# Gated outputs of two head groups parked in DRAM, and a key pair projected ahead of a gate, in a four-group decoder trunk

## The chip, the cores and the metric

One core of one Trainium2 chip runs the whole kernel. The time is in device microseconds of one launch. Each version was run three times; the median counts. The engines are called as in the profile: PE (TensorE), DVE (VectorE), ACT (ScalarE), POOL (GpSimd) and SP (SyncE, which issues all of this kernel's DMAs).

## The reference

Two layers, batch 1, 1024 tokens, 1024 channels. Each layer projects its input once, runs four groups of heads on slices of that projection, normalises each group's output, multiplies it by a gate and projects back:

```python
def hybrid_layer(x, pos, g_pre, w_in, sinks, conv_w, conv_b, g_cq, w_uq, g_ckv, w_ukv, g_grp, w_out, g_post):
    b, s, _ = x.shape
    h = rmsnorm(x, g_pre) @ w_in
    (a_q, a_k, a_v, b_b, b_c, b_x, c_q, c_kv, c_kr, d_q, d_k, d_v, gate) = jnp.split(h, SPLIT_IDX, axis=-1)
    ya = swa_sink_attention(...)          # A: sliding window, 4 heads of 64, 2 key heads
    yb = short_gated_conv(b_b, b_c, b_x, conv_w, conv_b)   # B: width 3, 256 channels
    yc = mla(c_q, c_kv, c_kr, pos, g_cq, w_uq, g_ckv, w_ukv)   # C: causal softmax, 4 heads
    yd = stick_breaking_attention(...)    # D: 4 heads of 64
    y = jnp.stack([ya, yb, yc, yd], axis=2)
    y = rmsnorm(y, g_grp.reshape(N_GROUPS, GROUP_WIDTH)).reshape(b, s, D_MIX)
    y = y * jax.nn.silu(gate)
    return x + rmsnorm(y @ w_out, g_post)

# D, for a block of 128 queries
z = einsum(q, k) * scale
log_keep = where(mask, log_sigmoid(-z), 0.0)
after = cumsum(log_keep, reverse=True) - log_keep
a = where(mask, exp(log_sigmoid(z) + after), 0.0)
out = einsum(a, v)
```

All of it is float32. Group D's cumulative sum along the keys is what makes its weights costly outside the matmuls.

## The kernel before, in words

A product in float32 is made of three passes: each operand is split into a rounded part (an ACT copy) and the rest (a subtraction on DVE or POOL), and PE multiplies high by high, high by low and low by high. A projection chunk, such as the 128 columns DK1 (the keys of D's second head pair), has 48 matmuls of 512 columns: two halves Q of 512 tokens, 8 slices of 128 input channels, three passes. The keys to what stands in such names: AQ, AK and AV are queries, keys and values of A, and likewise for D; G10 and G11 are the two 128-column chunks of group B's gate (groups are numbered A 0, B 1, C 2, D 3).

D's work comes in tasks, one for a head and 256 queries: scores into a bank `sc` (with a mask product), ACT's exponentials, on DVE a scan along the keys and a product with the break weights, for two query blocks each. Then PE transposes the weights into a bank `tr`, ACT copies their high and DVE subtracts their low part into a PT tile, and PE multiplies the values with it into the one bank `pv`.

The program is emitted by a planner (class `Weaver`). Each stage is a Python generator, here called a stream: `gemm()` (L1626) emits the projections, `scores()` the scores, `pvs()` the transposes and the products with values, `norms()` the group norms, `z_parts()` and `z_split` (L1487) the split of the gated outputs for the last projection, `w_out_rows()` the load of that projection's weights, and `outs()` the projection. A stream yields a condition: `need(...)` waits for a mark of another stream, `room(n)` for n free tiles, `W.when(...)` for the planned time at which data is there. `run()` goes on with the first stream in its list that could start by the planned present, else with the earliest. PE runs in the order of emission. On ACT, DVE, POOL and for SP's issues the planner keeps a list of planned slots, puts each instruction into the first hole that fits, and ties neighbours together, so that every engine has one fixed order.

SBUF tiles come from pools with fixed numbers: 34 `g` tiles of 4 KB per partition (activations, keys, outputs, split weights), 6 `P`, 3 `PT`, 3 weight tiles `W`, 2 `raw` buffers for weights that arrive, 3 `t`, 4 `f`. PSUM has 3 banks `sc`, 2 `tr`, 1 `pv` and 2 `w`.

In a layer the stream of projections goes: C's columns, B (all of it), DV, DQ0, DK0, C's gate (two chunks), DQ1, B's first gate chunk G10, DK1, G11, then A's AV, AQ0, AK0, AQ1, D's gate, A's gate. The order in which the weights arrive is a list of its own (L714 to L717), and has to be the same. `gate` (L1180) multiplies a group's normed output `L["y"][grp][Q]` by its gate in place on POOL. B's convolution output goes through DRAM (`yBd`) until its norm and again until its gate; C's, D's and A's outputs stay in SBUF. Each output tile holds one half Q of the tokens and takes one `g` tile; C's and B's four gated tiles are held until `z_split` rounds and splits them for the last projection.

Names in the profile: a tile or bank has its tag behind an x (`xg`, `xP`, `xPT`, `xsc`); `xw` is both the bank `w` and a weight tile `W`. All of ACT's, DVE's and POOL's instructions pass through one helper line, L85; matmuls are L479, transposes (as a product with `ident`) L483, DMA issues L396.

## Time and profile before

| | before |
|---|---|
| median of 3 runs | 1173.47 us (1171.46 to 1174.13) |
| the profiled execution's own time | 1172.81 us |
| its span, first to last instruction | 1171.0 us |
| mean granted clock of TensorE | 0.995 |
| instructions | 17883 |
| D's second pair, layer 0 | 321.2 to 408.5 us |
| D's second pair, layer 1 | 897.9 to 985.1 us |

The span lies within the time; 1.8 us are ahead of the first and behind the last instruction. "Busy" of PE counts each matmul from its start to its modelled end; neighbours overlap. The granted clock is a share of TensorE's full speed; it has two levels, 2.4 GHz (1.00) and 1.2 GHz (0.50), and a mean over a stretch lies between them.

### The profile page before, as it was taken

How to read it: one execution, taken by the hardware profiler on the slowest of the kernel's cores; microseconds unless marked ns; L12 is line 12 of the kernel's file. 1: busy time of each engine (PE TensorE's matmuls, PEld its weight loads, DVE VectorE, ACT ScalarE, POOL GpSimd, SP SyncE). 2: the span in 40 equal slices, each digit the busy share in tenths (PEclk: the TensorE clock that was granted, in tenths of full speed). 3: DMA queues.
4: the chain of work that ended last, by engine and by line, in shares of the span. 5: the costliest groups of instructions: out<-in, count | busy, mean ns of one | idle time of the engine just before them, and what ended most of it. 6: DMA issues, size and time to landing. Idle time of an engine off the chain costs nothing.

```text
span 1171.0 us, 17883 instructions
## 1 busy us (share of the span) xinstructions
PE 1142.7 (98%) x6302; PEld 978.2 (84%) x6302; DVE 822.9 (70%) x1685; ACT 640.1 (55%) x1443; POOL 347.9 (30%) x477
## 2 busy tenths in 40 slices
PE   8999999999999999999999999999999999999997
PEld 6988888987787788878889888899878877888886
DVE  6868687549969878852764777873688788888323
ACT  7665566246556667631454655651655565675211
POOL 4225143116224235310221332420353332451000
PEclk9999999999999999999999999999999999999999
DMA  6121202121111011321451122021201111124123
GB/s 227 36 64 33 68 19 60 50 81 27 27 37 37 18 37 52 98 73 46 161 166 29 37 54 55 19 82 36 76 25 37 27 28 28 28 64 155 61 72 126
DMA packets 72678, 71.98 MB, mean 61 GB/s; under 512 B 10062, under 2 KB 59276, under 8 KB 72588
## 3 DMA queue, kind: packets, MB, share of 16 engines
q1 hardware_dynamic: 72588, 70.83, 20.4%
q8 instruction: 50, 0.82, 0.3%
q14 instruction: 40, 0.33, 0.1%
HBM read 55.09 MB, written 11.53 MB: 57 GB/s over the span
## 4 chain that ended last, share of the span: by engine, by line
PE 73%; DVE 14%; ACT 5%; issue 4%; DMA 2%; POOL 1%; SPq 0%; DVEq 0%; POOLq 0%; ACTq 0%
PE xw L479 37%; PE xsc L479 22%; PE xtr L483 8%; DVE xP L85 7%; PE xpv L479 6%; DVE xg L85 3%; ACT xP L85 2%; DMA xP<-in_w_out_dram 1%; DVE xPT L85 1%; ACT xg L85 1%; DVE xs L85 1%; ACT xt L85 1%; DVE xt L85 1%; POOL xs L85 1%; DVE xw L85 1%
## 5 line engine op out<-in xcount | busy, mean ns | idle before, releaser
L479 PE MATMUL xw<-xg,xw 128*128 128x512 f32 x2064 | 516.7, 396 | 2.4 <-DVE xf L85 2.4
L479 PEld LDWEIGHTS xw<-xg,xw 128*128 128x128 f32 x2064 | 376.0, 188 | 75.3 <-DVE xf L85 3.3
L479 PE MATMUL xsc<-xg,xg 128*128 128x512 f32 (+7 forms) x1400 | 307.2, 364 | 0.3 <-ACT xP L85 0.2
L479 PEld LDWEIGHTS xsc<-xg,xg 128*128 128x128 f32 (+1 forms) x1400 | 239.0, 190 | 37.6 <-ACT xP L85 4.1
L85 POOL TENSOR_SCALAR xP<-xP,xs 128x256 f32<-128x256 f32 (+7 forms) x128 | 82.5, 656 | 161.7 <-DVE xs L85 113.5
L85 ACT CAST xPT<-xtr 128x512 fp32r<-128x512 f32 (+1 forms) x192 | 101.2, 550 | 49.7 <-PE xtr L483 48.1
L479 PE MATMUL xpv<-xPT,xg 128*128 128x256 f32 (+1 forms) x720 | 120.2, 290 | 7.0 <-DVE xPT L85 6.5
L483 PE MATMUL xtr<-ident,xP 128*128 128x128 f32 (+1 forms) x843 | 124.3, 275 | 2.7 <-DVE xP L85 1.5
L85 DVE TENSOR_TENSOR xPT<-xtr,xPT 128x512 fp32r<-128x512 f32 (+1 forms) x192 | 117.0, 630 | 11.3 <-ACT xPT L85 10.9
L479 PEld LDWEIGHTS xpv<-xPT,xg 128*128 128x128 f32 x720 | 103.2, 189 | 23.9 <-DVE xPT L85 13.6
L479 PE MATMUL xw<-xg,xg 128*128 128x416 f32 (+2 forms) x648 | 114.5, 326 | 0.0
L85 DVE TENSOR_TENSOR xg<-xw,xg 64x512 fp32r<-64x512 f32 (+1 forms) x112 | 62.9, 574 | 69.7 <-ACT xg L85 68.5
L85 ACT CAST xg<-xw 64x512 fp32r<-64x512 f32 (+1 forms) x112 | 53.4, 492 | 103.0 <-PE xw L479 92.5
L483 PEld LDWEIGHTS xtr<-ident,xP 128*128 128x128 f32 (+1 forms) x843 | 97.7, 141 | 14.2 <-DVE xP L85 3.5
L85 ACT ACTIVATE xP<-xP,xs 128x256 f32<-128x256 f32 (+7 forms) x128 | 80.7, 631 | 49.0 <-DVE xs L85 43.8
L85 POOL TENSOR_TENSOR xw<-xraw,xw 128x512 fp32r<-128x512 f32 x42 | 64.8, 1546 | 139.2 <-ACT xw L85 102.7
L479 PEld LDWEIGHTS xw<-xg,xg 128*128 128x128 f32 x648 | 102.0, 189 | 1.9
L85 DVE TENSOR_TENSOR_SCAN xP<-xP 128x128 f32<-128x128 f32 (+3 forms) x64 | 95.3, 1488 | 4.3 <-ACT xP L85 4.2
L85 POOL TENSOR_TENSOR xt<-xt 64x128 f32<-64x128 f32 x64 | 40.0, 626 | 153.1 <-DVE xt L85 124.6
L85 ACT ACTIVATE xP<-xsc 128x512 f32<-128x512 f32 (+2 forms) x192 | 80.1, 514 | 9.2 <-DVE xP L85 8.1
L85 ACT ACTIVATE xt<-xsc 128x512 f32<-128x512 f32 x32 | 19.2, 599 | 116.4 <-PE xsc L479 92.6
L85 ACT COPY xt<-xpv 64x512 f32<-64x512 f32 x80 | 46.7, 584 | 44.7 <-PE xpv L479 43.4
(128 smaller groups left out, 1291.9 us busy)
## 6 DMA issues: line engine op xcount, KB each, us to landing
xraw<-in_w_in_dram SPq DMA_DIRECT2D x96, 256.0 KB, 2.8
xP<-in_w_out_dram SPq DMA_DIRECT2D x16, 512.0 KB, 3.9
xg<-in_x_dram SPq DMA_DIRECT2D x8, 512.0 KB, 9.0
xg<-xP SPq DMA_DIRECT2D x32, 128.0 KB, 2.3
xP<-in_x_dram SPq DMA_DIRECT2D x8, 512.0 KB, 4.2
xP<-xs SPq DMA_DIRECT2D x8, 512.0 KB, 3.8
xs<-xP SPq DMA_DIRECT2D x7, 512.0 KB, 3.5
out_dram<-xP SPq DMA_DIRECT2D x7, 512.0 KB, 2.6
```

What stands on the lines that cost most here:

```text
L85: ins = real(*args, **kw)
L479: in_order(T.matmul(ps, lhs, rhs, start=start, stop=stop, skip_group_check=True))
L483: in_order(T.transpose(ps, src, idn))
```

## The change

Three edits, in both layers.

The chunk DK1 is emitted ahead of G10 instead of behind it, and its weights arrive in that order. It no longer waits for the scores of D's first pair. G10 and G11 follow one another, behind B's norm.

The four gated tiles of C (two) and B (two) go to DRAM as soon as their second gate chunk is multiplied in (`yd`, which takes the place of `yBd`), and their `g` tiles are released. `z_split` fetches each into a new tile, ahead of its split, when three `g` tiles are free; the stream then waits for the planned time of the landing.

A's two output tiles are allocated when two `g` tiles are free, and no longer only behind D's last product with values. B's normed tiles are fetched back behind DK1 (the mark `("D", l, 1)`) instead of behind DK0.

```diff
@@ w_tiles
-                "DQ0", "DK0", "G20", "G21", "DQ1", "G10", "DK1", "G11", "AV0", "AQ0", "AK0", "AQ1",
+                "DQ0", "DK0", "G20", "G21", "DQ1", "DK1", "G10", "G11", "AV0", "AQ0", "AK0", "AQ1",
@@ gate
-    def gate(L, grp, ms=(0, 1)):
+    def gate(L, grp):
+
         def ev(Q, pb):
             t = ftile()
             silu(t, pb)
             z = L["y"][grp][Q]
             G.tensor_tensor(z[:, m, :], z[:, m, :], t, ALU.mult)
             W.release(t)
+            if m and grp in L["yd"]:
+                dma(L["yd"][grp][Q], z)
+                W.release(z)
@@ z_split
     def z_split(L, grp, Q, wait=True):
-        z = L["y"][grp][Q]
         free = W.idle_from("V")
         ts = []
+        back = grp in L["yd"]
+        if back:
+            yield room(3)
+            L["y"][grp][Q] = gtile([P, 2, 512], F32)
+            dma(L["y"][grp][Q], L["yd"][grp][Q])
+        z = L["y"][grp][Q]
         for m in range(2):
             if wait:
-                yield lambda: (ts or W.room("g", 2, 34)) and max(0.0, free() - 4000.0)
+                yield lambda: (ts or W.room("g", 2, 34)) and max(
+                    0.0, free() - 4000.0, W.ready("A", [z]) if back else 0.0
+                )
@@ the layers' dicts
-                yBd=[dp.tile([P, 2, 512], F32, name=nm("yBd")) for _ in range(NQ)],
+                yd={g: [dp.tile([P, 2, 512], F32, name=nm("yd")) for _ in range(NQ)] for g in (1, 2)},
@@ gemm
             yield from d_q(L, 1)
-            yield need(("norm", l, 1, 1))
-            yield from gate(L, 1, (0,))
-            yield need(("scores", l, "D0"))
             yield from d_k(L, 1)
             W.mark("D", l, 1)
-            yield from gate(L, 1, (1,))
+            yield need(("norm", l, 1, 1))
+            yield from gate(L, 1)
             yield from a_v(L)
             yield from a_q(L, 0)
             yield need(("scores", l, "D1"))
             yield from a_k(L)
             yield from a_q(L, 1)
-            yield need(("pv", l, "D1", 1))
+            yield room(2)
             L["y"][0] = [gtile([P, 2, 512], F32) for _ in range(NQ)]
             W.mark("A", l)
@@ norms
-            yield need(("D", l, 0))
+            yield need(("D", l, 1))
             for Q in range(NQ):
                 yield room(1)
                 L["y"][1][Q] = gtile([P, 2, 512], F32)
-                dma(L["y"][1][Q], L["yBd"][Q])
+                dma(L["y"][1][Q], L["yd"][1][Q])
```

The other lines of the diff are renames of `yBd`.

Where instructions moved, DVE, layer 0, among the tasks of D's first pair. Before, 12 rows that end with the first scan of the second pair (`xP` 128x128; scans are printed as SCALAR_TENSOR_TENSOR with one operand); `xf` is the gate's tile, `xw<-xraw` the split of a weight, `xPT` the low part of transposed weights, `xg` 64x512 the evacuation of keys, `xg` 64x128 and `xt` that of products with values:

```order
L85 TENSOR_TENSOR xPT_3702<-xtr_3697,xPT_3702 128x512
L85 TENSOR_TENSOR xPT_3710<-xtr_3705,xPT_3710 128x512
L85 SCALAR_TENSOR_TENSOR xf_3716<-xf_3716,xw_3633 128x512
L85 TENSOR_TENSOR xw_3720<-xraw_3547,xw_3720 128x512
L85 TENSOR_TENSOR xPT_3739<-xtr_3734,xPT_3739 128x512
L85 TENSOR_TENSOR xPT_3750<-xtr_3746,xPT_3750 128x384
L85 TENSOR_TENSOR xg_2535<-xpv_3729,xt_3766 64x128
L85 TENSOR_TENSOR xt_3766<-xpv_3729,xt_3766 64x384
L85 TENSOR_TENSOR xg_3788<-xw_3725,xg_3787 64x512 x2
L85 TENSOR_TENSOR xg_3794<-xw_3725,xg_3793 64x512 x2
L85 TENSOR_TENSOR xg_3788<-xw_3799,xg_3787 64x512 x2
L85 SCALAR_TENSOR_TENSOR xP_3843<-xP_3843 128x128
```

And of the change, the 12 rows from the first evacuation of keys:

```order
L85 TENSOR_TENSOR xg_3632<-xw_3582,xg_3631 64x512 x2
L85 TENSOR_TENSOR xPT_3657<-xtr_3652,xPT_3657 128x512
L85 TENSOR_TENSOR xPT_3668<-xtr_3664,xPT_3668 128x384
L85 TENSOR_TENSOR xg_3638<-xw_3582,xg_3637 64x512 x2
L85 TENSOR_TENSOR xg_3632<-xw_3643,xg_3631 64x512 x2
L85 TENSOR_TENSOR xg_2539<-xpv_3647,xt_3721 64x128
L85 TENSOR_TENSOR xt_3721<-xpv_3647,xt_3721 64x384
L85 SCALAR_TENSOR_TENSOR xP_3743<-xP_3743 128x128
L85 TENSOR_TENSOR xg_3638<-xw_3643,xg_3637 64x512 x2
L85 TENSOR_TENSOR xPT_3732<-xtr_3727,xPT_3732 128x512
L85 TENSOR_TENSOR xPT_3740<-xtr_3735,xPT_3740 128x512
L85 TENSOR_TENSOR xP_3744<-xP_3744,xP_3743 128x127
```

The keys and the first scan come among the last PT tiles of the first pair, ahead of the gate's first evacuation.

PE, layer 0, at the group norm of A. Before, `xsc` from `xg` is the last projection and the two rows of L483 are the norm's transposes of the squared sums (`xt`) and of their root (`xs`); `xw` is A's gate:

```order
L479 MATMUL xw_5466<-xg_391,xw_5260 128x512 x3
L479 MATMUL xsc_5562<-xg_5386,xg_5233 128x512 x3
L479 MATMUL xsc_5562<-xg_5389,xg_5234 128x512 x3
L479 MATMUL xsc_5562<-xg_5394,xg_5239 128x512 x3
L483 MATMUL xtr_5572<-ident,xt_5535 128x128 x4
L479 MATMUL xsc_5562<-xg_5397,xg_5240 128x512 x3
L479 MATMUL xsc_5562<-xg_5402,xg_5253 128x512 x3
L479 MATMUL xsc_5562<-xg_5405,xg_5254 128x512 x3
L479 MATMUL xsc_5562<-xg_5542,xg_5378 128x512 x3
L483 MATMUL xtr_5593<-ident,xs_5577 128x128 x4
```

Of the change:

```order
L479 MATMUL xw_5537<-xg_390,xg_5191 128x512 x3
L483 MATMUL xtr_5547<-ident,xt_5499 128x128 x4
L479 MATMUL xw_5537<-xg_391,xg_5191 128x512 x3
L479 MATMUL xw_5537<-xg_392,xw_5280 128x512 x3
L479 MATMUL xw_5537<-xg_393,xw_5280 128x512 x3
L479 MATMUL xw_5537<-xg_394,xw_5280 128x512 x3
L479 MATMUL xw_5537<-xg_395,xw_5280 128x512 x3
L483 MATMUL xtr_5581<-ident,xs_5552 128x128 x4
L479 MATMUL xsc_5634<-xg_5466,xg_5243 128x512 x3
```

The last projection begins behind both transposes, and A's gate stands between them; 30 of its matmuls come between A's last product with values and the first transposes.

SP, layer 0, at the loads for the last projection. Before, `xraw` is a weight of the gates and `xP` a row pair of `w_out`:

```order
L396 DMA xraw_4997<-in_w_in_dram 128x4x128
L396 DMA xP_5384<-in_w_out_dram 128x2x512
L396 DMA xraw_5181<-in_w_in_dram 128x4x128
L396 DMA xraw_5221<-in_w_in_dram 128x416
L396 DMA xP_5392<-in_w_out_dram 128x2x512
L396 DMA xraw_5263<-in_w_in_dram 128x416
L396 DMA xP_5400<-in_w_out_dram 128x2x512
```

Of the change, with the reloads `xg<-xyd`:

```order
L396 DMA xraw_5005<-in_w_in_dram 128x4x128
L396 DMA xg_5241<-xyd_168 128x1024
L396 DMA xg_5249<-xyd_166 128x1024
L396 DMA xP_5464<-in_w_out_dram 128x2x512
L396 DMA xP_5472<-in_w_out_dram 128x2x512
L396 DMA xraw_5189<-in_w_in_dram 128x4x128
L396 DMA xraw_5194<-in_w_in_dram 128x416
L396 DMA xg_5297<-xyd_169 128x1024
L396 DMA xraw_5283<-in_w_in_dram 128x416
L396 DMA xg_5341<-xyd_167 128x1024
```

Two reloads come ahead of all of the rows of `w_out` and two among them and the weights.

## Rows read from the trace of the kernel before

**Rows 1.** Part 1 of the page: busy time of each engine, share of the span, instructions.

```profile
PE 1142.7 (98%) x6302; PEld 978.2 (84%) x6302; DVE 822.9 (70%) x1685; ACT 640.1 (55%) x1443; POOL 347.9 (30%) x477
```

**Rows 2.** The timeline of PE in layer 0, at four places. Columns: start, length of the run of alike instructions, engine, line, operation, out<-in, tile, shape, count, and in brackets the idle time before and what ended it.

```profile
386.43 0.23 PE L479 MATMUL xsc<-maskD,identb 128*128 128x128 bf16 x1
386.47 0.94 PE L479 MATMUL xw<-xg,xw 128*128 128x512 f32 x3
...
399.24 0.63 PE L479 MATMUL xpv<-xPT,xg 128*128 128x256 f32 x4
399.71 0.60 PE L483 MATMUL xtr<-ident,xP 128*128 128x128 f32 x4
400.06 0.72 PE L479 MATMUL xpv<-xPT,xg 128*128 128x256 f32 x4
...
505.42 0.65 PE L483 MATMUL xtr<-ident,xs 128*128 128x128 f32 x4
505.83 39.06 PE L479 MATMUL xsc<-xg,xg 128*128 128x512 f32 x171
```

**Rows 3.** PE's groups of instructions from 321.2 to 408.5 us, shapes kept apart: busy us, mean ns of one, idle before them and what ended it.

```profile
L479 PE MATMUL xw<-xg,xw 128*128 128x512 f32 x231 | 57.6, 397 | 0.0
L479 PE MATMUL xpv<-xPT,xg 128*128 128x256 f32 x79 | 13.3, 290 | 2.4 <-DVE xPT L85 2.3
L483 PE MATMUL xtr<-ident,xP 128*128 128x128 f32 x72 | 11.2, 285 | 0.2 <-DVE xg L85 0.2
L479 PE MATMUL xsc<-xg,xg 128*128 128x512 f32 x20 | 7.8, 473 | 0.1
L479 PE MATMUL xsc<-maskD,identb 128*128 128x128 bf16 x16 | 3.8, 236 | 0.0
L479 PE MATMUL xsc<-xg,xg 128*128 128x384 f32 x12 | 3.7, 396 | 0.0
L479 PE MATMUL xsc<-xg,xg 128*128 128x256 f32 x12 | 2.8, 312 | 0.0
L483 PE MATMUL xtr<-ident,xf 128*128 128x128 f32 x8 | 1.2, 273 | 0.0
L479 PE MATMUL xsc<-xg,xg 128*128 128x128 f32 x4 | 0.8, 270 | 0.0
```

**Rows 4.** Waits of PE over the span: us in total, times, longest.

```profile
PE xpv L479 <- DVE xPT L85: 6.5, 10, 2.1
```

**Rows 5.** The timeline of PE and of DVE at the longest of these waits, columns as in rows 2; between the first and the second row of DVE a product and a scan are left out.

```profile
392.64 0.28 PE L479 MATMUL xpv<-xPT,xg 128*128 128x256 f32 x1
395.01 0.51 PE L479 MATMUL xpv<-xPT,xg 128*128 128x256 f32 x2 [2.10 <-DVE xPT L85]
...
386.93 2.01 DVE L85 TENSOR_TENSOR_SCAN xP<-xP 128x896 f32<-128x896 f32 x1
...
392.44 2.05 DVE L85 TENSOR_TENSOR xP<-xP,xP 128x1023 f32<-128x1023 f32 x1
394.42 0.54 DVE L85 TENSOR_TENSOR xPT<-xtr,xPT 128x384 fp32r<-128x384 f32 x1
```

**Rows 6.** Windows of all engines: stretch, its us, busy us of PE, PEld, DVE, ACT and POOL (with counts), granted clock, DMA share, GB/s.

```profile
395.00:400.00 5.00, 4.99 (x24) 4.34 (x25) 3.97 (x7) 3.83 (x8) 1.92 (x3) 0.66 0.35 94
500.00:505.00 5.00, 3.80 (x20) 2.85 (x18) 4.93 (x9) 3.08 (x6) 0.95 (x1) 1.00 0.62 198
```

**Rows 7.** PE's groups as in rows 3, for layer 1, 897.9 to 985.1 us.

```profile
L479 PE MATMUL xpv<-xPT,xg 128*128 128x256 f32 x79 | 13.2, 289 | 2.5 <-DVE xPT L85 2.4
```

**Rows 8.** The timeline of DVE where DK1 is evacuated.

```profile
334.85 1.38 DVE L85 TENSOR_TENSOR xg<-xw,xg 64x512 fp32r<-64x512 f32 x2 [3.17 <-ACT xg L85]
...
337.48 1.40 DVE L85 TENSOR_TENSOR xg<-xw,xg 64x512 fp32r<-64x512 f32 x2 [1.24 <-ACT xg L85]
...
340.29 1.38 DVE L85 TENSOR_TENSOR xg<-xw,xg 64x512 fp32r<-64x512 f32 x2 [1.41 <-ACT xg L85]
```

**Rows 9.** Windows of DVE alone: stretch, its us, busy us of DVE, granted clock, DMA share, GB/s.

```profile
321.20:341.70 20.50, 11.97 (x21) 1.00 0.15 39
341.70:407.40 65.70, 58.19 (x73) 0.97 0.11 29
```

**Rows 10.** The timeline of DVE at the end of D: an evacuation for AQ0, the last PT subtractions, the last product of a scan.

```profile
394.99 1.39 DVE L85 TENSOR_TENSOR xg<-xw,xg 64x512 fp32r<-64x512 f32 x2
...
402.56 1.15 DVE L85 TENSOR_TENSOR xPT<-xtr,xPT 128x512 fp32r<-128x512 f32 x2
...
406.19 1.21 DVE L85 TENSOR_TENSOR xP<-xP,xP 128x1023 f32<-128x1023 f32 x1
```

**Rows 11.** The timeline of PE at the second transposes of D's norm.

```profile
430.84 0.65 PE L483 MATMUL xtr<-ident,xs 128*128 128x128 f32 x4 [0.46 <-POOL xs L85]
```

**Rows 12.** The timeline of PE at A's norm: the gate's last matmuls behind A's last product, the last projection's first, and the two sets of transposes.

```profile
497.11 1.60 PE L479 MATMUL xw<-xg,xw 128*128 128x512 f32 x6
498.55 2.21 PE L479 MATMUL xsc<-xg,xg 128*128 128x512 f32 x9
501.95 0.66 PE L483 MATMUL xtr<-ident,xt 128*128 128x128 f32 x4 [1.20 <-DVE xt L85]
502.36 2.98 PE L479 MATMUL xsc<-xg,xg 128*128 128x512 f32 x12
```

**Rows 13.** DMA issues: out<-in, queue, count, KB of each, median us from issue to landing.

```profile
xg<-xyBd SPq DMA_DIRECT2D x4, 512.0 KB, 4.2
```

## What the change is expected to do to the time

> **What bounds the kernel now.** I read the share of each engine first [rows 1]: TensorE is busy for 98% of the span. The change adds and removes no matmul, so it can only move the time that TensorE loses between matmuls. A matmul's record is longer than its step to the next one, and busy time therefore hides small waits; so I set a stretch's matmuls against their pace from start to start, its length against the sum. The paces [rows 2]: 39.06 us for 171 matmuls of 512 columns is 0.228 us each; transposes of 128 columns (399.71 to the next start and 505.42 to 505.83, four in 0.41) take 0.103; four products of 256 columns (399.24 to 399.71) 0.118 each; a mask product (386.43 to 386.47) 0.04.
>
> The stretch I care about runs from 321.2 to 408.5 us, in which group D's second key pair is made and scored in layer 0. Its counts [rows 3] make 251 x 0.228 + 12 x 0.171 (three quarters) + 91 x 0.118 + 84 x 0.103 + 16 x 0.04 = 79.3 us of work in 87.3 us: 8.0 us are lost. TensorE's waits name the loser: the products with the values (xpv) wait for VectorE to finish the low half of the transposed weights [rows 4]. The longest of them [rows 5] begins after 392.64 and ends at 395.01; on VectorE two scans and two products, 386.93 to 394.42 without a gap, stand ahead of the one 0.54 us subtraction that is wanted. Right behind it the granted clock is 0.66 over 395 to 400, against 1.00 in 500 to 505, where TensorE also waited, but for 1.20 us [rows 6]; so 5 x 0.34 = 1.7 us of the 8.0 are the clock at its lower level (1.2 instead of 2.4 GHz), behind a wait of 2.1 us. Layer 1 repeats it: the same 79 products, 2.5 us of idle before them [rows 7].
>
> Why is VectorE late there? Look at what it does before: it idles 3.17, 1.24 and 1.41 us for the keys' evacuation by ScalarE [rows 8], and is busy for 11.97 us of 20.5 between 321.2 and 341.7, and then for 58.19 of 65.7 [rows 9]. First it starves, because D's next scores need keys that are still being projected; then it is the bound of the stretch.
>
> Two smaller losses come later in each layer: the group norm of A, and the second half of D's norm (below).
>
> **The change part by part.**
>
> *Keys ahead of the gate.* DK1's 48 matmuls come before G10's 48 instead of behind them, so D's next scores start under the gate's matmuls. On VectorE all of the work from 321.2 to 407.4 stays except what now comes behind the last D product: four subtractions for AQ0 (two rows of 1.39), the last two PT subtractions (1.15) [rows 10], and one of A's turned values (some 0.6, as one of those): 11.97 + 58.19 - 2.8 - 1.2 - 0.6 = 65.6 us. On TensorE the order puts 39 matmuls of 512 columns (AK0's 27, 12 of AQ0) behind the point where the last D tile is transposed: 79.3 - 39 x 0.228 = 70.4 us. So VectorE has 65.6 us of work under 70.4, no longer 58.2 in a dense part of 65.7 behind a starved one. If VectorE idles as much as in that dense part (7.5 us), the stretch takes 73.1, and 2.7 us are lost; if not at all, none. If the scores, their PT tiles and the gate's evacuations collide as badly as before, 8.0. I take 3.0, near the row of the dense part, since the dependences are the same; 5.0 us are saved per layer, of which 1.7 are the clock, provided that no wait as long as 2 us stays.
>
> The rows show a second price of packing. The same VectorE product over 1023 columns took 2.05 us at 392.44 and 1.21 at 406.19 [rows 5, 10]. The Trainium skill (SBUF — State Buffer, Who interferes with whom) says that a VectorE instruction with two SBUF inputs and a GpSimd one that reads SBUF shut each other out for a whole instruction; that speaks against the change, which puts the same GpSimd work beside a fuller VectorE. If it met all four widest products of the stretch, three more hits of 0.84 us would bring the loss from 3.0 to 5.5, and the sum to 9 us saved instead of 14.
>
> *Group D's norm and A's output tiles.* A's output tiles no longer wait for D's last product, only for room, and the second transposes of D's norm, which stood between A's first scores and waited 0.46 us for GpSimd [rows 11], now stand 15 rows ahead of them under AK0. Gain 0 to 0.5; I take 0.5.
>
> *Group A's norm.* Before, 9 matmuls from 498.55 take 2.05 us, but TensorE goes on at 501.95: 1.35 us lost. Then 12 from 502.36 take 2.7, and it goes on at 505.42: 0.3 more [rows 2, 12]. In the new order the projection does not start between these transposes: 30 gate matmuls (6.8 us) stand ahead of the first four and 15 (3.4 us) between the two sets, where 6 + 9 (3.4 us) and 12 (2.7) stood. The chain took 501.95 - 497.11 = 4.8 us behind A's last products, where the gate's last 6 matmuls start [rows 12], and 505.42 - 502.36 = 3.1 us to the second; both are under the new cover. 1.7 us saved, 0 if other work on ScalarE or VectorE takes the cover.
>
> *The trips to DRAM.* Per layer four stores and four loads of 512 KB are new, all on SP. SP's own issue of them is beside other work. A store waits on SP for GpSimd's last gate product, and the weights behind it wait too; in the new queue it stands at least one weight transfer ahead of need, so I put it at nothing. A load of this size lands after 4.2 us [rows 13]. What waits is ScalarE's first cast of the reloaded tile, and behind it in its queue are the gate's tanh and the copies for A's products. Bounds: nothing, if every load is early, and 4 x 4.2 = 16.8 us per layer, if each is waited for in full by TensorE. The stream that emits the cast first waits for the planner's time of the landing, and B's old reload, the row's own kind, was issued long before use: I take 0.5 us per layer.
>
> *Sum.* 5.0 + 0.5 + 1.7 - 0.5 = 6.7 us per layer, 13.4 for two. The profiled execution took 1172.81 us (span 1171.0), so 1159.4 by its own time; it lies 0.66 us under the median of the runs, 1173.47, so a median of 1160.1.
>
> **The rivals.**
>
> *VectorE stays the bound.* 65.6 us under 70.4 is 93%, more than the 89% of the old dense part. Then the order only moves the waits: PT subtractions stand behind the scans as before, and the last third of the stretch loses 6 to 8 us again, the clock with it. Left are 0 to 2.0 + 0.5 + 1.7 - 0.5, or 1.7 to 3.7 per layer: 1166 to 1170. For it: the scans of a task still stand ahead of the former task's PT. Against it: the idle of rows 8 is gone, and the gate asks less of VectorE than AQ0 and AK0.
>
> *The reloads are late (slower).* ScalarE's queue is in order: a cast that waits for its load holds tanh and A's copies, and TensorE follows. The gain of 7.2 us per layer (sum without the trips) is used up at 1.8 us per reload. At 2.5 us, well under the landing, it is 10 per layer: 1173.5 + 2 x (10 - 7.2) = 1179. For it: the loads stand among w_out's rows on one queue and need free tiles. Against it: tiles of D are free by then.
>
> *It does not do what it says.* The waits could move to A's scores, where VectorE is also busy, and the loss be the same: 1172 to 1175.
>
> **How the numbers follow.** The forecast, 1154 to 1165, has 0.67; VectorE as the bound 0.18; no change 0.06; late reloads 0.09. What this kernel's timing can tell from no change is 0.2%, 2.3 us, so faster means under 1171.1: all of the first and nearly all of the second, 0.84; same 0.07; slower 0.09. The best case (nothing lost in the stretch, no price for the trips) is 2 x (8.0 + 0.5 + 1.7) = 20.4 us, 1153. The range 1154 to 1171 leaves out the slower and unchanged cases and a few hundredths of the best.
>
> **What would show it.** Right: VectorE's idle for keys gone and its busy share above 85% from the keys on; no granted clock under 1.00 near the end of D in either layer; no wait of xpv over 1.5 us; A's norm transposed without idle; ScalarE's casts of reloaded tiles without idle from DMA. Wrong: TensorE waiting for PT as long as before with VectorE full (the first rival), a ScalarE or TensorE wait that ends with a load from DRAM (the second), or new idle in A's scores (the third). A dip of the clock that stays in place would cost 1.7 us of each layer's 5.0.

## The result and the profile after

The changed kernel took 1167.28 us (median of 4 runs, 1166.5 to 1168.14) beside 1173.71 for the kernel before (4 runs): ratio 0.9948, 95% interval 0.9936 to 0.9960. That is 6.4 us less, where 13.4 were forecast. A second set of runs gave 0.9938 (0.9925 to 0.9950).

Part 1 of the page after, and TensorE's waits (us in total, times, longest); they answer to [rows 1] and [rows 4]:

```profile
PE 1138.8 (98%) x6302; PEld 976.0 (84%) x6302; DVE 822.2 (71%) x1683; ACT 638.0 (55%) x1443; POOL 357.3 (31%) x479
```

```profile
PE xpv L479 <- DVE xPT L85: 6.2, 14, 1.3
...
PE xtr L483 <- DVE xt L85: 1.1, 2, 0.5
...
PE xtr L483 <- POOL xs L85: 0.2, 1, 0.2
```

The wait for the PT tiles is shorter at its longest (1.3 us, 2.1 before) but there are 14 of them instead of 10, and the sum has hardly moved (6.2, 6.5 before). Windows of all engines, columns as in rows 6, two in layer 0 and one at the end of D in layer 1:

```profile
340.00:360.00 20.00, 18.69 (x100) 15.35 (x99) 19.38 (x24) 10.94 (x24) 10.70 (x10) 1.00 0.10 27
...
380.00:400.00 20.00, 19.91 (x119) 16.79 (x119) 16.64 (x23) 12.97 (x25) 2.65 (x6) 1.00 0.15 40
...
960.00:980.00 20.00, 20.00 (x121) 17.37 (x120) 17.69 (x24) 11.25 (x22) 3.19 (x4) 1.00 0.05 14
```

The granted clock is 1.00 where it was 0.66 [rows 6]. From 340 to 360 us VectorE (third busy figure) is full, 19.38 of 20 us, and TensorE is busy for 18.69 us, the least of any 20 us of layer 0 from 280 us on.

To find what each place still loses I set matmuls against the paces of rows 2 again, now from start to start of named matmuls. TensorE's groups in the change between the last product with values of D's first pair (334.16 us) and that of the second (406.09):

```profile
L479 PE MATMUL xw<-xg,xw 128*128 128x512 f32 x180 | 45.5, 398 | 0.0
L479 PE MATMUL xpv<-xPT,xg 128*128 128x256 f32 x74 | 12.9, 293 | 1.6 <-DVE xPT L85 1.6
L483 PE MATMUL xtr<-ident,xP 128*128 128x128 f32 x72 | 10.5, 273 | 0.0
L479 PE MATMUL xsc<-xg,xg 128*128 128x512 f32 x20 | 7.0, 429 | 0.1
L479 PE MATMUL xsc<-xg,xg 128*128 128x384 f32 x12 | 3.3, 358 | 0.0
L479 PE MATMUL xsc<-maskD,identb 128*128 128x128 bf16 x14 | 3.2, 230 | 0.0
L479 PE MATMUL xsc<-xg,xg 128*128 128x256 f32 x10 | 2.1, 291 | 0.0
...
```

Four small groups with 18 matmuls of 128 columns are left out. A window counts the products that overlap its edges; without the two at the edges there are 200 of 512 columns, 12 of 384, 82 of 256, 90 of 128 and 14 masks: 45.6 + 2.05 + 9.7 + 9.3 + 0.6 = 67.2 us of work in 71.9, so 4.8 are lost. The same sum for the kernel before (329.90 to 418.27 us, with 254, 12, 84, 92 and 16) is 80.0 in 88.4: 8.4 lost. The table does this at five places of layer 0; each starts where the last one ends. The first starts at DQ1's last matmul; the places end at the first pair's last product, the second pair's, the first transposes of A's weights, A's last product and the 61st matmul of the last projection. Below the first two rows stand the kernels of the experiments.

| us lost, layer 0 | end of D's first pair | D's second pair | to A's first transposes | A's products | A's norm | sum |
|---|---|---|---|---|---|---|
| before | 1.80 | 8.38 | 1.15 | 1.49 | 1.83 | 14.65 |
| the change | 2.61 | 4.76 | 1.14 | 1.63 | 1.04 | 11.19 |
| no_trips | 4.57 | 4.06 | 1.15 | 2.00 | 0.76 | 12.55 |
| trips_only | 1.80 | 8.32 | 1.15 | 1.48 | 1.75 | 14.49 |
| gate_short | 2.61 | 3.46 | 1.15 | 1.67 | 1.04 | 9.93 |
| gate_dve | 2.62 | 4.36 | 1.23 | 1.66 | 1.03 | 10.89 |
| gate_dve_bc | 6.57 | 3.60 | 1.18 | 1.64 | 1.04 | 14.03 |
| gates_later | 2.61 | 4.05 | 2.03 | 1.65 | 1.03 | 11.36 |
| rows_late | 2.62 | 4.74 | 1.17 | 1.61 | 9.03 | 19.18 |
| product_short | 1.31 | 3.15 | 1.15 | 1.65 | 1.00 | 8.26 |
| split_dve | 1.74 | 2.48 | 1.68 | 1.63 | 1.00 | 8.53 |
| split_gate_dve | 1.75 | 2.93 | 1.19 | 1.64 | 1.01 | 8.52 |
| split_more | 5.34 | 2.47 | 1.65 | 1.64 | 1.01 | 12.12 |
| model | 2.21 | 4.02 | 2.12 | 0.88 | 0.12 | 9.35 |
| model_gate_dve | 2.17 | 3.43 | 1.90 | 0.84 | 0.12 | 8.46 |
| model_split | 1.78 | 5.06 | 0.82 | 0.84 | 0.12 | 8.62 |
| model_split_gate | 1.76 | 2.34 | 1.73 | 0.84 | 0.12 | 6.80 |

Layer 1 has 14.40 before and 11.23 in the change, so both layers together save 3.46 + 3.17 = 6.6 us, against 6.4 in the spans (1171.0 and 1164.6) and in the medians. In layer 0 D's second pair gains 3.6 us and A's norm 0.8, and 0.8 are given back at the end of the first pair. In the four kernels called model the projection begins earlier, and its 61st matmul comes ahead of the norm's second transposes; carried past these, A's norm loses 0.2 us there.

A loss in the table need not be a wait. I took the second pair's loss in layer 0 apart by the start of each matmul: before, 3.0 us are waits of TensorE, 1.7 the low clock and 3.6 small steps; in the change 2.0, 0 and 2.8. What the steps are is shown below, behind split_dve.

### The profile page after: what moved, and what is told of

Same layout as the page of the kernel before. It is cut to its first block, busy times and chain, and to the rows that moved or that the text cites. A ratio compares the mean times of both kernels' runs of the same rounds, so it can differ in the third digit from the quotient of the medians.

```text
span 1164.6 us, 17945 instructions
## 1 busy us (share of the span) xinstructions
PE 1138.8 (98%) x6302; PEld 976.0 (84%) x6302; DVE 822.2 (71%) x1683; ACT 638.0 (55%) x1443; POOL 357.3 (31%) x479
## 4 chain that ended last, share of the span: by engine, by line
PE 78%; DVE 13%; ACT 4%; issue 3%; POOL 1%; DMA 0%; DVEq 0%; SPq 0%; POOLq 0%; ACTq 0%
PE xw L479 40%; PE xsc L479 23%; PE xtr L483 8%; PE xpv L479 7%; DVE xP L85 7%; DVE xg L85 2%; DVE xPT L85 2%; ACT xP L85 1%; ACT xt L85 1%; ACT xg L85 1%; DVE xt L85 1%; DVE xf L85 1%; DMA xg<-in_w_in_dram 0%; ACT xPT L85 0%; DVE xs L85 0%
## 5 line engine op out<-in xcount | busy, mean ns | idle before, releaser
L479 PE MATMUL xsc<-xg,xg 128*128 128x512 f32 (+7 forms) x1400 | 304.0, 362 | 0.2
L483 PE MATMUL xtr<-ident,xP 128*128 128x128 f32 (+1 forms) x843 | 123.1, 273 | 2.6 <-DVE xP L85 1.5
L483 PEld LDWEIGHTS xtr<-ident,xP 128*128 128x128 f32 (+1 forms) x843 | 96.7, 140 | 12.9 <-DVE xP L85 3.4
L85 POOL TENSOR_TENSOR xw<-xraw,xw 128x512 fp32r<-128x512 f32 x40 | 59.6, 1492 | 155.3 <-ACT xw L85 129.7
L85 POOL TENSOR_TENSOR xs<-xs,mhalf 128x1 f32<-128x1 f32 (+2 forms) x36 | 34.2, 949 | 131.1 <-DVE xs L85 131.1
```

The lines of the kernel that those rows point to most:

```text
L85: ins = real(*args, **kw)
L479: in_order(T.matmul(ps, lhs, rhs, start=start, stop=stop, skip_group_check=True))
L483: in_order(T.transpose(ps, src, idn))
```

## The experiments

Each ratio is to the kernel before on the same chip (medians 1175.47, 1174.85, 1174.91 and 1174.91 us for the four sets); every diff is against the changed kernel unless it says otherwise. The first set had the changed kernel in it again:

> The changed kernel once more, beside the others on one chip, so that they have it to stand against. Both theories: 1166.5 to 1168.2 us, the range it had.

Measured: 1167.81 us, 0.9938 (0.9925 to 0.9950). Its losses in layer 0 agree with those of the first trace within 0.05 us at every place.

**The edit's parts.** A's early output tiles need no run: with the old condition (`need(("pv", l, "D1", 1))`) in the place of `room(2)`, the program is the same, so this edit does nothing here. The trips and the order were taken apart.

```diff
-            if m and grp in L["yd"]:
+            if m and grp in L["park"]:
-        back = grp in L["yd"]
+        back = grp in L["park"]
```

`park` is an empty tuple in each layer's dict here.

> DK1 ahead of G10 as in the change, but the gated tiles of C and B stay in SBUF (no stores, no reloads). Theory 1 (the order alone makes the gain, and the trips only put work among A's products): the waits of A's products for PT at 470 and 474 us go, and the time is 1 to 2 us under the change. Theory 2 (the trips make room, and by that the cover over A's norm): A's norm loses 1.5 us or more per layer again, and the time is 1 to 2.5 us above the change, some 1169. D's stretch loses as much as in the change (near 5 us by pace) by either.

Measured: 1169.01 us, 0.9948 (0.9935 to 0.9962).

trips_only keeps the trips, and puts back the order, the loops and the weights' list of the kernel before.

> G10 ahead of DK1 as before, with the trips to DRAM of the change. Theory 1: D's stretch loses its 8 us per layer as before, with the clock's dip; the time is that of before or up to 1 us above it (the trips' price). Theory 2: A's norm loses under 1 us per layer in place of 1.65, and the time is 1 to 2.5 us under before.

Measured: 1174.53 us, 0.9988 (0.9980 to 0.9997). With the old order D's second pair loses 8.32 us, all that it lost before, and the sum of layer 0 is 14.49 against 14.65. So in the traces the trips bring 0.1 to 0.2 us per layer (by the medians 0.9 us over both), and the order the rest; theory 1 holds as to that. no_trips has the time that theory 2 gave it, but not for its reason: A's norm loses 0.76 there, less than in the change, so the cover over it comes from the order and not from the trips. Neither theory foresaw what else no_trips shows: its second pair is better and the end of its first pair worse, by a wait that the change hasn't (TensorE's scores for a ScalarE result), and in layer 0 by 1.7 us of low clock behind that wait:

```profile
PE xsc L479 <- ACT xP L85: 3.5, 2, 1.7
```

Without the trips the planner's order differs from the change's in D too, so no_trips is no clean measure of them; trips_only is, since TensorE's order differs from that of before only in A's part, behind D.

**What D's second pair still loses.** The longest wait for a PT tile in the change, on TensorE, VectorE and GpSimd (columns as in rows 2):

```profile
344.57 0.28 PE L479 MATMUL xpv<-xPT,xg 128*128 128x256 f32 x1
346.16 0.51 PE L479 MATMUL xpv<-xPT,xg 128*128 128x256 f32 x2 [1.31 <-DVE xPT L85]
...
340.79 1.40 DVE L85 TENSOR_TENSOR xP<-xP,xP 128x383 f32<-128x383 f32 x1
342.11 1.48 DVE L85 TENSOR_TENSOR_SCAN xP<-xP 128x512 f32<-128x512 f32 x1
343.69 1.95 DVE L85 TENSOR_TENSOR xP<-xP,xP 128x511 f32<-128x511 f32 x1
345.56 0.55 DVE L85 TENSOR_TENSOR xPT<-xtr,xPT 128x384 fp32r<-128x384 f32 x1
...
350.32 0.56 DVE L85 TENSOR_TENSOR xP<-xP,xP 128x383 f32<-128x383 f32 x1
...
352.11 0.67 DVE L85 TENSOR_TENSOR xP<-xP,xP 128x511 f32<-128x511 f32 x1
...
339.29 2.48 POOL L85 TENSOR_TENSOR xg<-xg,xf 128x512 f32<-128x512 f32 x1 [2.01 <-DVE xf L85]
...
342.58 1.26 POOL L85 TENSOR_TENSOR xg<-xt 64x128 f32<-64x128 f32 x1
343.80 1.28 POOL L85 TENSOR_TENSOR xw<-xraw,xw 128x512 fp32r<-128x512 f32 x1
...
360.53 1.28 POOL L85 TENSOR_TENSOR xg<-xg,xf 128x512 f32<-128x512 f32 x1
```

The product over 383 columns takes 1.40 us beside GpSimd's gate product and 0.56 alone; that over 511 takes 1.95 beside a sum of outputs and a weight's subtraction, and 0.67 alone. GpSimd's gate product takes 2.48 instead of 1.28. These 2.1 us of VectorE stand right ahead of the 0.55 us subtraction for which TensorE waits 1.31. The Trainium skill (SBUF — State Buffer, Who interferes with whom) says that a VectorE instruction with two SBUF inputs contends with a GpSimd one that reads SBUF, and the trace agrees by these lengths. By the same section an instruction with at most one SBUF input is not touched, and the trace agrees there too: VectorE's evacuations of keys and queries, with one operand in PSUM, take 690 ns each, half of what two take in rows 8 (1.38 to 1.40 us), and over the whole trace the 20 that overlap a GpSimd instruction by 0.3 us or more take 690 ns, the other 60 take 688. The group from 324 to 402 us:

```profile
L85 DVE TENSOR_TENSOR xg<-xw,xg 64x512 fp32r<-64x512 f32 x8 | 5.5, 690 | 0.5 <-ACT xg L85 0.3
```

To test that it costs time, the gate products were cut:

```diff
-            G.tensor_tensor(z[:, m, :], z[:, m, :], t, ALU.mult)
+            if grp == 1:
+                short(G, nc.gpsimd, z[:, m, :], z[:, m, :], t, ALU.mult)
+            else:
+                G.tensor_tensor(z[:, m, :], z[:, m, :], t, ALU.mult)
```

`short` gives the planner the full operation and issues it on the first 8 columns, so B's outputs stay ungated. (The kernel has four lines more, and its products are printed as L483.)

> The change, but GpSimd's product of group B's tile by its gate covers 8 of 512 columns (the rest of B's outputs stays ungated); the order on every engine is the same. Contention theory (GpSimd's instructions hold up VectorE's products of two SBUF operands): VectorE's product over 383 columns behind 340 us takes 0.6 instead of 1.40, the wait of 1.31 us at 344.57 falls under 0.7, and the time is 1 to 2.5 us under the change. Rival (VectorE simply has too much queued ahead of that PT tile): that wait stays within 0.3 us of 1.31, and the time within 0.5 us of the change.

Measured: 1164.12 us, 0.9905 (0.9892 to 0.9919). At the same place in its trace:

```profile
340.93 0.74 DVE L85 TENSOR_TENSOR xP<-xP,xP 128x383 f32<-128x383 f32 x1
341.59 2.72 DVE L85 TENSOR_TENSOR_SCAN xP<-xP 128x512 f32<-128x512 f32 x1
344.42 0.69 DVE L85 TENSOR_TENSOR xP<-xP,xP 128x511 f32<-128x511 f32 x1
...
345.63 0.50 PE L483 MATMUL xpv<-xPT,xg 128*128 128x256 f32 x2 [0.61 <-DVE xPT L85]
...
341.95 1.28 POOL L85 TENSOR_TENSOR xw<-xraw,xw 128x512 fp32r<-128x512 f32 x1
```

The contention theory holds: the wait falls to 0.61, and the stretch's loss by 1.3 us per layer (4.76 to 3.46). The medians of this set differ by 3.7 us (1 to 2.5 were expected). Of these 2.6 are this; the rest is not the edit's as far as the traces show, since the profiled runs differ by 1.6 us ahead of layer 0's first matmul of 512 columns already (66.1 us in change_again, 64.5 here). What is left at this place is the weight's subtraction, which now meets the scan: 2.72 us instead of 1.48. So the next set moved work off GpSimd.

```diff
-            G.tensor_tensor(z[:, m, :], z[:, m, :], t, ALU.mult)
+            (V if grp == 1 else G).tensor_tensor(z[:, m, :], z[:, m, :], t, ALU.mult)
```

> The change, with group B's products of tile and gate on VectorE instead of GpSimd (4 per layer). Contention theory (shown in part by the shortened products: 3.7 us less): VectorE has 4 x 0.65 us more of its own work per layer, but its products of scores and break weights are no longer held up by these four; 1 to 3 us under the change. Rival (the shortened products helped because z was stored earlier or GpSimd was free for other work, and VectorE is the bound by its sum of work): 1 to 4 us above the change, as 2.6 us per layer are added to an engine that is busy for 19.4 of 20 us from 340 to 360.

Measured: 1166.65 us, 0.9929 (0.9915 to 0.9943); the interval overlaps the change's. The second pair gains 0.4 us in layer 0 in place of the 1.3 of the cut products. VectorE has four new products of 0.7 to 1.1 us, and the wait at this place stays: it is 1.42 us, as two subtractions of weights on GpSimd (1.28 us each) now hold up the scan over 512 columns (2.73 us) and the product over 511 behind it (1.59). With `grp != 3` in place of `grp == 1`:

> As the one before, with group C's products of tile and gate on VectorE too (they fall among the tasks of D's first pair). Contention theory: 0 to 2 us under the former. Rival: 1 to 3 us above it.

Measured: 1171.81 us, 0.9967 (0.9956 to 0.9979); a miss, 5 us above the former. The end of the first pair loses 6.57 us: with four more products on VectorE there, TensorE's projections wait 2.76 us for an evacuation by VectorE, and in layer 0 the clock falls behind it (1.6 us).

The next kernel moves the gate, and the weights' list with it:

```diff
-            yield need(("norm", l, 1, 1))
-            yield from gate(L, 1)
             yield from a_v(L)
             yield from a_q(L, 0)
+            yield need(("norm", l, 1, 1))
+            yield from gate(L, 1)
```

> The change, with G10 and G11 behind AV0 and AQ0, so that GpSimd's products of B's gate meet the end of D's second pair or A's keys instead of its middle. Contention theory: the wait near 344 us falls, but AQ0's evacuations (8 x 0.69 us per layer on VectorE) take the gates' place (4 x 0.68 us); the time stays within 2 us of the change, either way. Rival (VectorE's sum of work is the bound): 2 to 5 us above the change.

Measured: 1168.84 us, 0.9946 (0.9933 to 0.9960). As expected, it is within 2 us of the change: the second pair gains 0.7 us, and 0.9 are lost behind it.

The subtractions of weights were the other part:

```diff
-            W.sooner((G, V), m, raw, t).tensor_tensor(
+            e = V if key in ("G10", "G11", "AV0", "AQ0") else W.sooner((G, V), m, raw, t)
+            e.tensor_tensor(
```

> The change, with the subtractions of the weights of G10, G11, AV0 and AQ0 on VectorE always, where a planned end chose between it and GpSimd. A subtraction is 0.68 us on VectorE and 1.28 on GpSimd. Contention theory: what VectorE takes over (0.68 us each) is about what GpSimd's instruction cost it by holding it up (0.8 us where it meets a product): within 1 us of the change. Rival (VectorE's sum of work): 1 to 3 us above.

Measured: 1163.29 us, 0.9904 (0.9886 to 0.9921), better than expected: some 4 us under the change (0.0034 of 1175), with no overlap of the intervals. VectorE and TensorE at the place of the 1.31 us wait, and the total of these waits:

```profile
343.74 1.48 DVE L85 TENSOR_TENSOR_SCAN xP<-xP 128x512 f32<-128x512 f32 x1
345.32 0.69 DVE L85 TENSOR_TENSOR xP<-xP,xP 128x511 f32<-128x511 f32 x1
345.93 0.55 DVE L85 TENSOR_TENSOR xPT<-xtr,xPT 128x384 fp32r<-128x384 f32 x1
...
347.06 0.52 PE L479 MATMUL xpv<-xPT,xg 128*128 128x256 f32 x3
```

```profile
PE xpv L479 <- DVE xPT L85: 2.0, 8, 0.4
```

VectorE does the subtraction itself in 0.68 us and is rid of delays of 1.2 to 1.3. Scan and product have their own lengths again, and TensorE doesn't wait there; the waits for PT fall from 6.2 us to 2.0. Both pairs gain, 0.9 and 2.3 us in layer 0; 0.5 is lost again behind them.

The 2.48 us that the second pair still loses here are no waits that the profile shows: it has none of TensorE in this stretch (from 0.15 us on), in either layer. They are steps. Three matmuls of 512 columns behind a mask product, and the next start:

```profile
340.45 0.94 PE L479 MATMUL xw<-xg,xw 128*128 128x512 f32 x3
341.24 0.49 PE L483 MATMUL xtr<-ident,xP 128*128 128x128 f32 x3
```

By the pace they take 0.68 us, and they take 0.79. In layer 0's second pair 34 steps are some 0.09 us over their pace, 31 of them at the first matmul of a run of alike ones, 3.0 us in sum; all other steps together are 0.5 under theirs. The paces come from long runs of alike matmuls, where such steps hardly occur. What makes them, small hidden waits or the turn to other operands, these runs do not show. Of the 4.76 us that the change loses in this stretch, VectorE's lateness is thus the 2.0 of waits, and moving the subtractions takes all of it.

How far can VectorE be unloaded? Its product of weights and scan was cut in the same way as the gate:

```diff
-            V.tensor_tensor(bt[:, 0 : w - 1], bt[:, 0 : w - 1], kt[:, 1:w], ALU.mult)
+            short(V, nc.vector, bt[:, 0 : w - 1], bt[:, 0 : w - 1], kt[:, 1:w], ALU.mult)
```

> The change, but VectorE's product of break weights and scans covers 8 columns of each row (the rest of D's weights lacks its product; the order of every engine is the same). About 17 us per layer of VectorE's work in D go, with all that GpSimd can hold up of them. If VectorE's queue is what D's second stretch still loses by (4.25 us per layer from the first pair's last product to the second's), the loss falls to 1 to 2 us, the waits of xpv for PT fall from 6.1 us to under 2, and the time by 5 to 8 us. If the chain through ScalarE and the banks is (rival), the loss stays above 3.5 and the time within 2 us.

Measured: 1156.78 us, 0.9849 (0.9832 to 0.9866). The time falls by some 10 us (0.0089 of 1175), more than the 5 to 8 of the queue theory, and the waits for PT fall to 1.8 us as it has it; but the second pair still loses 3.15 us (2.6 in layer 1), between the two expectations. Much of the gain is elsewhere: from DQ0's first matmul to DQ1's last 2.1 us are lost in place of 4.4. In layer 1 TensorE has no wait left in the second pair, so the last 2.6 us there are the steps again, which no run here removes.

Two kernels had a planner that counts the overlap:

```diff
+        if key == "V" and not bank and op in ("tensor_tensor", "tensor_tensor_scan"):
+            at = self.place(key, t, dur, False)
+            dur += max([s[1] - max(s[0], at) for s in self.busy["G"] if s[0] < at + dur and at < s[1]], default=0.0)
         t = self.place(key, t, dur)
```

> The change, with a planner that lengthens a planned scan or a product of two SBUF operands on VectorE by what it overlaps of a planned GpSimd instruction, so that its order takes account of being held up. If the remaining loss of D's stretches is an order made with too short times, the time is 1 to 4 us under the change; if VectorE has no room whatever the order is, within 1 us; a worse order elsewhere can cost 2 us.

Measured: 1164.98 us, 0.9921 (0.9906 to 0.9936); the interval overlaps the change's.

> The planner of the one before, and group B's products of tile and gate on VectorE. Expected by the contention theory: the best of these kernels, 2 to 5 us under the change; by the rival, above the one before by 1 us or more.

Measured: 1162.86 us, 0.9900 (0.9883 to 0.9917). This one is clear of the change. In the table their gain in the second pair is small (0.7 and 1.3 us), 1.0 and 0.8 are lost again on the way to A's first transposes, and ahead of all this, from DQ0's first matmul to DQ1's last, the first loses more (6.1 us, 4.4 in the change), 1.7 of it by the clock behind a wait of 2.44 us. The rest of what they win is outside D: A's products (0.88 and 0.84 in place of 1.63) and A's norm (0.12 in place of 1.04). The expectation looked for it in D's stretches alone.

Four more kernels put these together:

> The change, with both the subtractions of four chunks' weights and group B's gate products on VectorE. If what is left of the stretch's loss with the subtractions moved (2.0 us per layer) is GpSimd's gate products, it falls to about 1 and the time by 1 to 2 us under the kernel with the subtractions alone; if VectorE is full by its own work, 0 to 2 us above it.

Measured: 1163.10 us, 0.9896 (0.9880 to 0.9911): the same as with the subtractions alone. In neither kernel does the profile show a wait of TensorE in the second pair, so the theory's "falls to about 1" could not come: what is left are steps. With the subtractions off GpSimd the gate products cost the same on either engine.

> The change, with the subtractions of the weights of G20, G21, DQ1 and DK1 on VectorE too. These fall among the tasks of D's first pair, where 4.2 us per layer are lost up to DQ1's last matmul. If GpSimd's subtractions are behind that as well, it falls to 2 to 3 us, and the time by 2 to 4 us under the kernel with four chunks moved; if VectorE's sum of work or the single pv bank is, no gain, or 1 to 2 us above.

Measured: 1165.62 us, 0.9922 (0.9910 to 0.9935), 2.3 us above split_dve. The edit adds `"G20", "G21", "DQ1", "DK1"` to its list of keys. The part from DQ0 to DQ1 gains 1.5 us per layer (2.9 lost), as the theory has it, but the end of the first pair loses 5.34 by a new wait of the projections for a VectorE evacuation and 1.6 us of low clock behind it. The wait over both layers, where VectorE is too full again as in gate_dve_bc:

```profile
PE xw L479 <- DVE xg L85: 6.0, 3, 2.8
```

> The planner that counts GpSimd's overlaps, with the four chunks' subtractions on VectorE. If the two gains add (4.5 and 2.8 us under the change on their chips): 1160 to 1162; if the planner only avoided the same collisions: as the better one alone, 1163.

Measured: 1161.83 us, 0.9885 (0.9867 to 0.9903). The sum is in the range of two gains that add, but not by their places: the second pair loses 5.06 us here, more than in the change, by a new wait of 1.70 us of D's norm's transposes for VectorE, and the gains are at the end of the first pair and at A.

> As the one before, with B's gate products on VectorE too: 1159 to 1162 if GpSimd's products still hold VectorE up there, else 1 us or more above the one before.

Measured: 1159.00 us, 0.9861 (0.9847 to 0.9875). This is the fastest of the kernels that leave nothing out (the intervals of it and of the one before overlap); it loses 6.80 us in layer 0 where the kernel before loses 14.65 and the change 11.19, the least in the second pair (2.34, without a wait in the profile) and nearly nothing at A's norm.

**A's norm.** The change there, on TensorE, ScalarE and VectorE:

```profile
485.74 4.99 PE L479 MATMUL xw<-xg,xw 128*128 128x512 f32 x21
490.57 2.20 PE L479 MATMUL xw<-xg,xg 128*128 128x512 f32 x9
493.31 0.66 PE L483 MATMUL xtr<-ident,xt 128*128 128x128 f32 x4 [0.54 <-DVE xt L85]
...
487.34 2.18 ACT L85 CAST xg<-xP 128x512 fp32r<-128x512 f32 x4
489.54 0.58 ACT L85 COPY xt<-xpv 64x512 f32<-64x512 f32 x1
...
488.16 2.98 DVE L85 TENSOR_TENSOR xg<-xP,xg 128x512 fp32r<-128x512 f32 x3
491.17 0.69 DVE L85 TENSOR_TENSOR xg<-xpv,xt 64x512 f32<-64x512 f32 x1
```

A's last product is done when the gate's matmuls go on at 485.74. ScalarE takes up its evacuation (`xt<-xpv`) at 489.54, behind four casts of `w_out` rows, and VectorE the rest of it at 491.17, behind three of their subtractions. The first transposes come at 493.31, 7.6 us behind the product, where the kernel before had 4.8 [rows 12]. A run held these rows' splits back (the cut shows the place; the call of `wout_rows` becomes `yield from wout_rows`):

```diff
dma(raw, w_out[L["l"], k * P : (k + 2) * P, c].rearrange("(k p) c -> p k c", p=P))
+        if not hf:
+            yield need(("pv", L["l"], "A", 1))
```

> The change, with the rounding and splitting of w_out's first four row pairs held back until A's last products are emitted (their loads stay where they are). Theory: the casts and subtractions of these rows, which stand ahead of A's evacuation and squares on ScalarE and VectorE, take the cover over A's norm; without them the waits at 492.6 (0.69 us) and 497.1 (0.25 us) go, and the time is 1 to 2 us under the change if the rows are still there for the projection. Rival (the chain of the norm itself is as long as the cover): these waits stay within 0.3 us. By either, rows that come too late for the projection show as a new wait of the first xsc matmuls for xg.

Measured: 1183.26 us, 1.0063 (1.0048 to 1.0079). Its trace:

```profile
488.75 0.59 ACT L85 COPY xt<-xpv 64x512 f32<-64x512 f32 x1
...
487.04 5.00 PE L479 MATMUL xw<-xg,xw 128*128 128x512 f32 x21
491.88 0.60 PE L483 MATMUL xtr<-ident,xt 128*128 128x128 f32 x4
...
506.55 2.02 PE L479 MATMUL xsc<-xg,xg 128*128 128x512 f32 x3 [4.25 <-ACT xg L85]
```

Half of the theory is shown: the evacuation comes 1.7 us behind 487.04 instead of 3.8, and the first transposes at 4.8 us without a wait. But the rows are late for the projection, which waits 4.25 us, more than the norm ever lost, and 3.3 us go to the low clock around that wait. So the time does not test the theory, only the trace does. A better place for these rows is ahead of A's last products, as in the kernels with the changed planner (the fastest of them, with three lines more, so that its products are L482):

```profile
500.65 3.65 PE L482 MATMUL xsc<-xg,xg 128*128 128x512 f32 x15
504.14 0.60 PE L486 MATMUL xtr<-ident,xt 128*128 128x128 f32 x4
```

There the projection (`xsc`) has begun before A's last products, its rows are split by then, and the chain of the norm takes 3.5 us under 15 matmuls.

## Why the prediction was right in direction and twice too large

- **What bounds.** Right: the whole gain is time lost between matmuls, most of it in D's second pair, where the products wait for VectorE's PT subtraction.
- **Keys ahead of the gate.** Priced at 5.0 us per layer; measured 2.8 (1.80 + 8.38 lost before, 2.61 + 4.76 after). The old 2.1 us wait and the low clock are gone, as forecast; the clock's 1.7 us are nearly half of what the second pair gains. The step that failed is "I take 3.0, near the row of the dense part": some 5.2 of the 8.0 stay (by the table's marks 5.6 of 8.4). VectorE's idle time was taken for the measure of what is lost. What the runs showed in its place has three parts: 2.0 us of waits for PT tiles, which come from VectorE's instructions that GpSimd makes longer (gate_short and split_dve); some 2.8 us of small steps of TensorE, which are no waits that the profile shows and which the sum of 8.0 counted as loss that an order could remove; and 0.8 us at the end of the first pair, where DK1's evacuations now stand among the last PT tiles and which the prediction had at nothing. So "if not at all, none" and the best case of 20.4 us were out of reach: split_dve and model_split_gate lose 2.5 and 2.3 us without a wait of TensorE in the profile. The paragraph's own second sum, 5.5, is near the 5.2 in part by luck: its mechanism, products held up by GpSimd, is the one that was shown, but it put 2.5 us on these hits beside 3.0 of idle time. (Its "9 us saved instead of 14" leaves out the trips; with them it is 8.4 instead of 13.4.)
- **D's norm.** Priced at 0.5, measured 0. Its wait for GpSimd went (1.1 us over both layers before, 0.2 after), but the way to A's first transposes loses 1.14 us as before (1.15): 10 of the small steps stand there where 4 were. A's early tiles can't be the reason for any of it, as they change no order.
- **A's norm.** Priced at 1.7, measured 0.8. The step that failed is that a chain of 4.8 us lies under the new cover: the chain itself became 7.6 us long, by `w_out` rows in front of it on ScalarE and VectorE. The lower bound, other work that takes the cover, was named and not chosen.
- **The trips.** Priced at 0.5 against; in the change A's products lose 0.14 more, and trips_only puts the whole of the trips at 0.1 to 0.2 us gained. No load was waited for.
- **Sum.** 2.8 + 0 + 0.8 - 0.1 = 3.5 us in layer 0, not 6.7.
- **The rivals.** The time, 1167.3, is in the band given to VectorE as the bound (1166 to 1170). Its sign came in part: VectorE is full from 340 to 360 us, and TensorE's waits for PT add up to 6.2 us, 6.5 before. But its mechanism kept the old long wait and the clock's dip, and both are gone. Late reloads did not come.

## What to carry to other kernels

An engine's share of busy time hides instructions that another engine makes longer: compare the same operation at two places before trusting its mean. A sum of matmuls against their pace in long runs finds more than waits: here some 2.5 us of it stayed where the profile showed no wait of TensorE, so take the loss apart before pricing what an order can win. Where GpSimd and VectorE can both do a subtraction, choose by what the choice delays, since 1.28 us on an idle GpSimd can cost the full VectorE more than the 0.68 us of doing it itself; and stop where VectorE has no room. When cover is found for a chain, look at what is queued ahead of the chain on each engine it crosses.

## What the runs showed of the hardware that was not expected

The scan is held up by GpSimd as the products are, and for longer (2.72 us for 512 columns beside a weight's subtraction, 1.48 without).

The forecast made the return of the clock hang on no wait of 2 us being left. In model TensorE waits 2.44 us in layer 0, and the granted clock is 0.66 over the next 5 us:

```profile
293.94 0.96 PE L482 MATMUL xw<-xg,xw 128*128 128x512 f32 x3 [2.44 <-DVE xf L85]
```

```profile
295.00:300.00 5.00, 5.00 (x27) 4.58 (x26) 2.02 (x4) 0.91 (x2) 0.25 (x1) 0.66 0.26 105
```

In model_split_gate a matmul at the same place waits as long, and the clock stays at 1.00:

```profile
294.46 0.98 PE L482 MATMUL xw<-xg,xw 128*128 128x512 f32 x3 [2.44 <-DVE xf L85]
```

```profile
280.00:300.00 20.00, 17.56 (x101) 14.55 (x100) 17.44 (x22) 11.48 (x27) 8.80 (x6) 1.00 0.25 79
```

In no_trips it falls behind a shorter wait, 1.75 us (0.66 from 310 to 315 us), shorter than the 2.10 behind which it fell before [rows 5, 6]. So the length of one wait alone does not decide it; what does is not settled by these runs.
